# Attention keeps both parts of the split input x in DRAM, and the gated linear attention heads load them

## The chip, the cores and the metric

The kernel runs on one core of a Trainium2 chip. A core has TensorE (PE, the matrix unit), VectorE (DVE), ScalarE (ACT), GpSimd (POOL) and SyncE (SP, which here only issues DMAs); each takes its own instructions in order, and semaphores tie them together. Data lies in on-chip SBUF (128 partitions), matmul results in PSUM, inputs and outputs in DRAM. The metric is device time in microseconds (us); less is better.

## The reference, cut to what matters

One inference layer over 2048 prompt tokens and 64 sample tokens (8 sequences of 8), width 1024, all fp32:

```python
z = jnp.einsum('btd,dn->btn', x, w_in)
q, k, v, g_att, gq, gk, gv, g_gla, g_lr, r_att, r_gla = jnp.split(z, SPLIT_POINTS, axis=-1)
...
    o_att, new_k, new_v = swa_prompt(q, k, v, attn_sink, rel_table)
...
log_a = jax.nn.log_sigmoid((jnp.einsum('btr,rk->btk', g_lr, w_gk_up) + b_gk).astype(jnp.float32)) / GATE_NORMALIZER
o_gla, S = gla(...)
...
h_att = jnp.einsum('bta,ad->btd', o_att * jax.nn.silu(g_att), w_pa)
h_gla = jnp.einsum('btv,vd->btd', o_gla * jax.nn.silu(g_gla), w_pg)
merged = jax.nn.sigmoid(r_att) * h_att + jax.nn.sigmoid(r_gla) * h_gla
y = jnp.einsum('btd,de->bte', merged, w_o)
x = layer_norm(DN_ALPHA * x + y, ln_g, ln_b)
```

`swa_prompt` is attention over a window of 128 with 8 query heads on 2 key heads; `gla` is gated linear attention with 4 heads, keys of 128, values of 256, scanned along the tokens. x is needed for the attention projections, again for those of each GLA head, and again for the merge gates.

## The kernel before

**Numbers.** A product of fp32 accuracy is made of three matmuls in a faster format: an operand is split into a rounded part `hi` and the rest `lo`, and hi·hi, hi·lo and lo·hi are summed in PSUM. `split` (L114 to 116) makes the parts: ACT casts to `hi` (L115), DVE, or POOL where told, subtracts for `lo` (L116). Weights are split too, by `wload` (L125): SP loads a 128x1024 tile into one of two staging buffers (`wst`), ACT makes `wh`, DVE `wl`.

**Stages.** The 2112 tokens are cut into six chunks (`CHUNKS`, L42: four of 384, then 256 and 320, the last with the 64 sample tokens). (1) Attention, L566 to 656: for each chunk the steps k, v, q0 to q3, gl (the low-rank gate), ga0 to ga3 (output gates), each a product (`proj`, L176) of 24 matmuls. After a step, `tick()` runs what a side queue holds for it: the scores, transposes and outputs of the chunk before or of this one. The last chunk's steps also call `wload()`, which brings the GLA weights. (2) GLA, L892 to 972: 4 heads times 6 chunks, each with the gate, values, k, q and two output gates. (3) Merge passes, L1115 to 1242: four passes (`w_pa`, `w_ra`, `w_rg`, `w_pg`) of 7 products of half size with 3 token units each and 4 groups of output rows (p0 to p3). `issue_w` and `issue_x` issue the loads (`ws`, `xc`), `make_w` and `make_x` split them, ahead of the unit that uses them. (4) The output product with layer norm.

**Where x comes from.** x lies transposed in DRAM (`xT`), as eight row tiles of 128. In attention, at ga1, `fetch_x` loads the next chunk's eight tiles, four into `u` units and four into `xst` staging, and at ga2 `part_x` splits them into 16 tiles of tag `x` (of 20); from chunk 1 on, every second subtraction goes to POOL. In GLA the same is done for every head and chunk: `fetch_x` at L939, `part_x` at L963. For the last chunk POOL also copies the sample columns (L158).

**What sets the order.** PE's order is the order of the program (`manual_schedule`, L62); on the other engines the framework's scheduler orders instructions by when they can run. Tile pools decide which SBUF bytes a tile gets, and the first instruction that writes a tile waits for the last users of those bytes. Working tiles come from tags: `u` (29 units of 1.5 KB a partition), `w` (26 of 4 KB), `x`, `xst`, `wst`. The merge stage opens two new pools (L1040): a left one, and a right one that holds `ws`, `xc`, `a12`, `fin`; their tiles lie on what the GLA stage held. PSUM has three `pd` buffers for the projections and five `pa` buffers.

**Names of the prediction.** In the last attention chunk `att_keys` (L334) evicts the k product from its `pd` buffer: ACT makes `kd0` and `kd1` (L340, 341), DVE `kl0` and `kl1` (L343, 344, twice), ACT two more `kd` (L345, 346), and L583 copies `kT`. q1 takes that same buffer. `pT` are transposed probabilities, copied by ACT (L410) and DVE (L408). `gla_store` (L786) writes a head's result `sg` to DRAM, from SP, but for the last chunk of the last head from POOL. The lines around the product and its use of PSUM:

```python
def step(ps_use, w=None):
    if w is not None:
        ps = pd()
        proj(ps[:, :T], w, x, T)
        ps_use(ps[:, :T])
    if last:
        wload()
    tick()
```

Of the kernel before, what the change touches and what calls it, by code (L numbers as in the profile page):

```python
# [12 lines left out]
F32 = mybir.dt.float32  # L13
F32R = mybir.dt.float32r
# [7 lines left out]
P = 128  # L22
D = 1024
# [6 lines left out]
G = 4  # L30
# [13 lines left out]
MT = 352  # L44
MS = NT // (2 * MT)
LB = 384
NU = 29
NX = 20


@with_exitstack
def kernel(ctx, tc, io):
# [17 lines left out]
        return psa.tile([P, 512], F32, tag="pa", name="pa")  # L70

    def wtile(dt=F32, name="w"):
        return sb.tile([P, D], dt, tag="w", name=name, bufs=26)

    def stile(name):
        return sb.tile([P, D], F32, tag="s", name=name, bufs=2)
# [1 line left out]
    def unit(dt=F32, name="u"):  # L78
        return sb.tile([P, TM], dt, tag="u", name=name, bufs=NU)

# [8 lines left out]
    xc_d = dram.tile([4, P, MS, KT // 2, MT], F32, name="xc_d")  # L89
    ac_d = dram.tile([4, P, MS, 2, MT], F32, name="ac_d")  # L90
    uc_d = dram.tile([4, P, MS, KT // 2, MT], F32, name="uc_d")
    gl_d = dram.tile([96, NT], F32, name="gl_d")
    bs_d = dram.tile([NH, P, LB], F32, name="bs_d")

# [19 lines left out]
    def split(dst_h, dst_l, src, eng=nc.vector):  # L114
        pin["a"] = nc.scalar.copy(dst_h, src)  # L115
        i = eng.tensor_tensor(dst_l, src, dst_h.bitcast(F32), ALU.subtract)  # L116
        if eng is nc.vector:
            pin["d"] = i
# [20 lines left out]
            wload()  # L139
        return wready.popleft()  # L140

    def xnew():
        return sb.tile([P, TM], F32R, tag="x", name="x", bufs=NX)

    def xstage():
        return sb.tile([P, TM], F32, tag="xst", name="xst", bufs=4)

    def fetch(src, k, t0, T, stage=xstage):
        st = stage()
        nc.sync.dma_start(st[:, :T], src[:, k, t0:t0 + T])  # L150
        return st, T

    def part(f, new=xnew, eng=nc.vector, samples=False):
        st, T = f
        hi, lo = new(), new()
        split(hi[:, :T], lo[:, :T], st[:, :T], eng)
        if samples:
            nc.gpsimd.tensor_copy(hi[:, T:T + NS], lo[:, T - NS:T])  # L158
        return hi, lo

    def load_split(src, k, t0, T, new):
        return part(fetch(src, k, t0, T), new)

    def fetch_x(src, t0, T):

        return [fetch(src, k, t0, T, unit if k < KT // 2 else xstage) for k in range(KT)]

    def part_x(fs, share=False, samples=False):

        return [part(f, eng=nc.gpsimd if share and k % 2 else nc.vector, samples=samples)  # L170
                for k, f in enumerate(fs)]

    def load_x(src, t0, T, stage=xstage, samples=False):
        return [part(fetch(src, k, t0, T, stage), samples=samples) for k in range(KT)]

    def proj(ps, w, x, T, mid=False):  # L176

# [48 lines left out]
    st, hi, lo = sb.tile([P, D], F32, tag="wst", name="wst", bufs=2), wtile(F32R, "wh"), wtile(F32R, "wl")  # L226
    wseq[0] = 1
    wready.append((hi, lo))
    x = []
    for k in range(KT):  # L230
        if k % 2 == 0:
            cs = slice(k * P, (k + 2) * P)
            nc.sync.dma_start(st[:, cs], io["wt"][0, :, cs])
            split(hi[:, cs], lo[:, cs], st[:, cs])
        x.append(part(fetch(io["xT"], k, *CHUNKS[0], unit)))
    wload(2)


# [314 lines left out]
    for c, (t0, T) in enumerate(CHUNKS):  # L553
        last = c == len(CHUNKS) - 1
        Tp = T - (NS if last else 0)
        nblk = Tp // W
        if last:
            wcap(16)
        A = {"kprev": kprev, "vprev": vprev, "q": [], "sil": []}

        def wt1(key):
            if c == 0:
                W1[key] = wget()
                wload()
            return W1[key]
# [11 lines that stand above are left out]
            gin = gate_in(0, 0)  # L577

        def keys(ps):
            att_keys(A, ps[:, :Tp], Tp)  # L580
            if last:
                A["kT"] = unit(name="kT")
                nc.scalar.copy(A["kT"][:, :T], ps)  # L583

        step(keys, wt1("k"))

        vT = unit(name="vT")
        vt = unit(name="vt").rearrange("p (b c) -> p b c", b=3)
        A["vT"], A["vt"] = vT, vt

        def vtrans(vT=vT, vt=vt, nblk=nblk):
            tp = pa()
            for i in range(nblk):
                nc.tensor.transpose(tp[:, i * P:(i + 1) * P], vT[:, i * P:(i + 1) * P], ident)
            nc.vector.tensor_copy(vt[:, :nblk].rearrange("p b c -> p (b c)"), tp[:, :nblk * P])

        step(lambda ps: nc.scalar.copy(vT[:, :T], ps), wt1("v"))
        at(1, vtrans)
        if c == 0:
            setup0()  # L600
            at(1, setup1)
            at(2, setup2)
            at(4, setup3)

        if last:
            A["qs"] = unit(name="qs")[:, :NB * G * TS].rearrange("p (b g t) -> p b g t", g=G, t=TS)
        for g in range(G):
            def queries(ps, g=g):
                att_queries(A, g, ps[:, :Tp], Tp)
                if last:  # L610
                    nc.scalar.mul(A["qs"][:, :, g, :], ps[:, Tp:].rearrange("p (b t) -> p b t", t=TS), HD ** -0.5)

            step(queries, wt1(("q", g)))

        lag = 2 if c == 0 else 0
        for bi in range(nblk):
            o = lag + 1 + 3 * bi
            at(o, lambda A=A, bi=bi: att_scores(A, bi, 0))
            at(o + 1, lambda A=A, bi=bi: att_scores(A, bi, 1))
            at(o + 3, lambda A=A, bi=bi: att_trans(A, bi, 0))  # L620
            at(o + 4, lambda A=A, bi=bi: att_trans(A, bi, 1))
            at(o + (6 if last and bi else 5), lambda A=A, bi=bi: att_out(A, bi))
        o = lag + 1 + 3 * (nblk - 1) + 5
        if last:
            at(0, lambda A=A, Tp=Tp: samp_rows(A, Tp))
            at(o - 5, lambda A=A, Tp=Tp: samp_prep(A, Tp))
            at(o - 3, lambda A=A: samp_keys(A))
            at(o - 1, lambda A=A, Tp=Tp: samp_scores(A, Tp, 0))
            at(o, lambda A=A, Tp=Tp: samp_scores(A, Tp, 1))
            at(o + 2, lambda A=A, Tp=Tp: (samp_trans(A, 0), samp_trans(A, 1)))  # L630
            at(o + 3, lambda A=A, Tp=Tp: samp_out(A, Tp))
# [12 lines left out]

        for g in range(G):
            sil = unit(name="sil")
            A["sil"].append(sil)
            w = wt1(("ga", g))
            if g == 1:
                with tc.issue_after(pin["w"].ins) if c == 0 else nullcontext():  # L650
                    xf = fetch_x(io["xT"], *CHUNKS[(c + 1) % len(CHUNKS)])
            if g == G - 2:
                xn = part_x(xf, share=(c > 0))
            step(lambda ps: gate(sil, ps, T), w)
        x = xn
        kprev, vprev = (A["k"], T), vt[:, nblk - 1]


# [233 lines left out]
    for h in range(GH):  # L892
        W2 = {}
        wcap(16 + 6 * h)
        for c, (t0, T) in enumerate(CHUNKS):
# [40 lines left out]
                    wload()  # L936
                tick()
            end = last and h == GH - 1
            xf = None if end else fetch_x(io["xT"], *CHUNKS[(c + 1) % len(CHUNKS)])  # L939
            ps = pd()  # L940
            proj(ps[:, :T], wt2("k"), x, T)
            gla_k(B, ps[:, :T])
# [15 lines left out]
            for m in range(2):  # L958
                sg = unit(name="sg")
                B["sg"].append(sg)  # L960
                w = wt2("g", m)
                if m == 0 and not end:
                    xn = part_x(xf, samples=(c + 1 == len(CHUNKS) - 1))  # L963
                ps = pd()
                proj(ps[:, :T], w, x, T, mid=end)
                gate(sg, ps[:, :T], T)
                if len(CHUNKS) - 4 < c < len(CHUNKS) - 1 and m == 1:
                    wload()
                tick()
# [207 lines left out]
    def load_m(t, u, n, last=False, queue=nc.sync):  # L1177
# [7 lines left out]
            out.append((st, n + NS * last))  # L1185
        return out

    def rest_m(t, u, n, last):
        return [part(f, onew, samples=last) for f in load_m(t, u, n, last)]

# [15 lines left out]
    for n, (q, i, s) in enumerate(units):  # L1206
# [16 lines left out]
        for p in range(NP4):  # L1223
# [12 lines left out]
            if n == len(units) - 1:  # L1236
                if p < 3:
                    xr0.append(load_xr(runs(1, p * P, P)))
                x += [part(f, onew) for f in xf[2 * p:2 * p + 2]]
        if n == len(units) - 2:  # L1240

            xf, x, xr0 = load_m(1, 0, TM, queue=nc.scalar), [], []
# [196 lines left out]
```

## Time and profile before

| what | value |
|---|---|
| median of 3 runs (lowest to highest) | 1845.85 us (1841.35 to 1847.47) |
| the profiled execution, its span | 1846.22 us, 1844.4 us |
| mean granted TensorE clock | 0.992 |
| busy: DVE, ACT, POOL | 1280.9 (69%), 849.9 (46%), 422.3 us (23%) |
| DMA | 315.84 MB, mean 171 GB/s |
| the five longest-running groups of matmuls by line: L185, L186, L187, L1233, L1232 | 409.1, 403.5, 403.1, 381.3, 381.4 us |

A row of groups has busy us, mean ns of one, the idle time of the engine just before, and what ended most of it. In a row of waits stand the total, the number of times and the longest. In a timeline row stand start, duration, engine, line, operation, and in brackets the idle time ahead with its releaser. Matmuls are pipelined: where each shows 0.31 us they may start 0.15 us apart, so their pace is read from the starts.

### The profile page before, as it was taken

Reading aid. Unit: us, or ns where it says so; the run is one execution under the profiler, and the core shown is the slowest. Engines: PE = TensorE matmul, PEld = TensorE weight load, DVE = VectorE, ACT = ScalarE, POOL = GpSimd, SP = SyncE. Lnnn points to the kernel's source line nnn. Section 1 sums busy time; section 2 is a strip of 40 time slices with the busy share of each in tenths; the row PEclk is TensorE's granted clock in tenths of the full one; section 3 lists DMA queues with packets and bytes.
Section 4 is the critical chain, followed back from the end, with each engine's and each line's share of the span. In section 5 each row is a group of like instructions: output and inputs, shape, how many; then the busy total and the mean of one; then the engine's idle time right before and its main releaser. Section 6 shows DMA issues by size and latency. Waiting matters only on the chain.

```text
span 1844.4 us, 32399 instructions
## 1 busy us (share of the span) xinstructions
PE 1807.9 (98%) x11683; PEld 1722.2 (93%) x11683; DVE 1280.9 (69%) x2662; ACT 849.9 (46%) x1947; POOL 422.3 (23%) x559
## 2 busy tenths in 40 slices
PE   8999999999999999999999999999999999989997
PEld 7998988899999999999999999999999999988886
DVE  5677778767776776777667669648657566966655
ACT  5444545645665565656546453435443543211110
POOL 3310111300110111011110243430355153631111
PEclk9999999999999999999999999999999999999998
DMA  7211013534345444543543189858887967895531
GB/s 233 63 56 38 12 47 100 165 131 156 120 148 170 143 143 144 186 132 107 181 145 119 58 274 315 283 178 292 276 311 256 310 216 245 287 312 177 166 111 41
DMA packets 199554, 315.84 MB, mean 171 GB/s; under 512 B 21453, under 2 KB 161189, under 8 KB 199376
## 3 DMA queue, kind: packets, MB, share of 16 engines
q1 hardware_dynamic: 192624, 304.61, 50.5%
q0 software_dynamic: 5616, 7.58, 1.5%
q8 instruction: 92, 1.51, 0.3%
q10 hardware_dynamic: 1152, 1.57, 0.3%
q14 instruction: 70, 0.57, 0.1%
HBM read 228.52 MB, written 86.14 MB: 171 GB/s over the span
## 4 chain that ended last, share of the span: by engine, by line
PE 91%; DVE 3%; DMA 3%; issue 1%; POOL 1%; SPq 0%; ACT 0%; DVEq 0%; ACTq 0%; POOLq 0%
PE pd L185 11%; PE pd L187 11%; PE pd L186 11%; PE pa L1234 9%; PE pa L1233 9%; PE pa L1232 9%; PE pd L199 7%; PE pd L198 7%; PE pd L200 7%; PE pa L421 2%; DMA cs<-tt_d 1%; PE pa L406 1%; PE pa L755 1%; PE pa L753 1%; PE pa L754 1%
## 5 line engine op out<-in xcount | busy, mean ns | idle before, releaser
L185 PE MATMUL pd<-x,wh 128*128 128x384 f32 (+2 forms) x1248 | 409.1, 328 | 7.0 <-ACT x L115 6.3
L186 PE MATMUL pd<-x,wh 128*128 128x384 f32 (+2 forms) x1248 | 403.5, 323 | 0.6 <-DVE x L116 0.3
L187 PE MATMUL pd<-x,wl 128*128 128x384 f32 (+2 forms) x1248 | 403.1, 323 | 0.6 <-DVE wl L116 0.6
L1233 PE MATMUL pa<-xl,wh 128*128 128x352 f32 x1176 | 381.3, 324 | 7.9 <-DVE xl L116 7.6
L1232 PE MATMUL pa<-xh,wh 128*128 128x352 f32 x1176 | 381.4, 324 | 2.6 <-ACT xh L115 2.3
L1234 PE MATMUL pa<-xh,wl 128*128 128x352 f32 x1176 | 381.9, 325 | 0.0
L185 PEld LDWEIGHTS pd<-x,wh 128*128 128x128 f32 x1248 | 236.5, 190 | 17.2 <-issue 8.9
L186 PEld LDWEIGHTS pd<-x,wh 128*128 128x128 f32 x1248 | 236.5, 190 | 2.0 <-DVE x L116 1.5
L187 PEld LDWEIGHTS pd<-x,wl 128*128 128x128 f32 x1248 | 236.1, 189 | 1.0 <-DVE wl L116 1.0
L1233 PEld LDWEIGHTS pa<-xl,wh 128*128 128x128 f32 x1176 | 222.7, 189 | 10.4 <-DVE xl L116 10.1
L1232 PEld LDWEIGHTS pa<-xh,wh 128*128 128x128 f32 x1176 | 222.5, 189 | 3.6 <-ACT xh L115 2.6
L1234 PEld LDWEIGHTS pa<-xh,wl 128*128 128x128 f32 x1176 | 224.5, 191 | 0.0
L116 DVE TENSOR_TENSOR xl<-xs,xh 128x1408 fp32r<-128x1408 f32 x63 | 110.5, 1753 | 69.4 <-ACT xh L115 35.7
L198 PE MATMUL pd<-wh,x 128*128 128x256 f32 x512 | 147.9, 289 | 0.0
L199 PE MATMUL pd<-wh,x 128*128 128x256 f32 x512 | 145.6, 284 | 1.2 <-DVE x L116 1.1
L200 PE MATMUL pd<-wl,x 128*128 128x256 f32 x512 | 144.6, 282 | 0.0
L115 ACT CAST x<-xst 128x384 fp32r<-128x384 f32 (+2 forms) x164 | 78.2, 485 | 139.9 <-PE pd L199 117.9
L115 ACT CAST xh<-xs 128x1408 fp32r<-128x1408 f32 x63 | 86.5, 1372 | 103.9 <-PE pa L1234 81.7
L746 POOL TENSOR_SCALAR sq<-sq 128x1 f32<-128x1 f32 (+1 forms) x68 | 21.4, 314 | 467.2 <-ACT ring L745 467.2
L199 PE MATMUL pd<-woh,x 128*128 128x512 f32 x256 | 101.5, 396 | 0.0
L198 PE MATMUL pd<-woh,x 128*128 128x512 f32 x256 | 101.5, 396 | 0.0
L200 PE MATMUL pd<-wol,x 128*128 128x512 f32 x256 | 101.5, 396 | 0.0
(318 smaller groups left out, 3683.6 us busy)
## 6 DMA issues: line engine op xcount, KB each, us to landing
wst<-wt SPq DMA_DIRECT2D x33, 512.0 KB, 3.6
xs<-xc_d SPq DMA_DIRECT2D x24, 704.0 KB, 5.6
cs<-tt_d SPq DMA_DIRECT2D x48, 352.0 KB, 4.7
u<-xT SPq DMA_DIRECT2D x84, 192.0 KB, 4.0
xst<-xT SPq DMA_DIRECT2D x76, 192.0 KB, 2.6
xs<-xT SPq DMA_DIRECT2D x18, 704.0 KB, 5.9
ws<-w_ra SPq DMA_DIRECT2D x36, 256.0 KB, 4.4
ws<-w_rg SPq DMA_DIRECT2D x36, 256.0 KB, 5.6
```

The lines of the kernel that those rows point to most:

```text
L115: pin["a"] = nc.scalar.copy(dst_h, src)
L116: i = eng.tensor_tensor(dst_l, src, dst_h.bitcast(F32), ALU.subtract)
L185: mm(ps, hi[:, s], xh[:, :T], start=(k == 0), stop=False)
L186: mm(ps, hi[:, s], xl[:, :T], start=False, stop=False)
L187: mm(ps, lo[:, s], xh[:, :T], start=False, stop=(k == n - 1))
L198: mm(ps, xh[:, xs], hi, start=(k == 0), stop=False)
L199: mm(ps, xl[:, xs], hi, start=False, stop=False)
L200: mm(ps, xh[:, xs], lo, start=False, stop=(k == KT - 1))
L421: mm(ot[pr, :], vb[:, pr], A["pT", bi, kv][:, hf], start=(hf == h0), stop=(hf == 1))
L1232: mm(ps, wh[:, ks], xh[:, ts], start=(k == 0), stop=False)
L1233: mm(ps, wh[:, ks], xl[:, ts], start=False, stop=False)
L1234: mm(ps, wl[:, ks], xh[:, ts], start=False, stop=(k == q.kh - 1))
```

## The change

x is split once, in attention, and its parts are stored to DRAM (`xs_d`, one tensor a chunk); GLA loads them.

- A slot of tag `x` is now 6 KB a partition and holds the `hi` and `lo` parts of two row tiles; there are 8 slots in place of 20 tiles (`NX`). `fetch_x` brings a chunk's raw x into two such slots (tag `x`, four row tiles each, by four DMAs), and `part_x` splits pair by pair. All subtractions are on DVE. The `xst` staging tag is gone from this stage.
- `keep_x`, called after the k step of each attention chunk, stores the four slots (4 DMAs of 768 KB for a chunk of 384).
- `load_x` takes the place of `fetch_x` and `part_x` in GLA, and of the last attention chunk's fetch: four DMAs of both parts.
- `u` units go from 29 to 24, `w` tiles from 26 to 25.
- `part` moves to the output stage, unchanged.

PE's instructions and their order are the same in both kernels.

```diff
-NU = 29
-NX = 20
+NU = 24
+NX = 8
+def xwide(c):
+    return 2 * CHUNKS[c][1] + (NS if c == len(CHUNKS) - 1 else 0)
...
-        return sb.tile([P, D], dt, tag="w", name=name, bufs=26)
+        return sb.tile([P, D], dt, tag="w", name=name, bufs=25)
...
+    xs_d = [dram.tile([4, P, 2 * xwide(c)], F32, name=f"xs{c}_d") for c in range(len(CHUNKS))]
...
+    def xslot(dt, name):
+        return sb.tile([P, 4 * TM], dt, tag="x", name=name, bufs=NX)
+    def xnew(c):
+        T, n = CHUNKS[c][1], xwide(c)
+        t = xslot(F32R, "x")[:, :2 * n]
+        v = t.rearrange("p (k w) -> p k w", k=2)
+        return t, v[:, :, :n - T], v[:, :, n - T:]
...
+    def fetch_x(c):
+        t0, T = CHUNKS[c]
+        out = []
+        for k in range(0, KT, 4):
+            st = xslot(F32, "xst")[:, :4 * T].rearrange("p (k t) -> p k t", k=4)
+            for j in (0, 2):
+                nc.sync.dma_start(st[:, j:j + 2], io["xT"][:, k + j:k + j + 2, t0:t0 + T])
+                out.append(st[:, j:j + 2])
+        return out
+    def part_x(c, sts):
+        T = CHUNKS[c][1]
+        out = []
+        for st in sts:
+            t, hi, lo = xnew(c)
+            split(hi[:, :, :T], lo, st)
+            if c == len(CHUNKS) - 1:
+                nc.gpsimd.tensor_copy(hi[:, :, T:], lo[:, :, T - NS:])
+            out.append((t, hi, lo))
+        return out
+    def keep_x(c, x):
+        for i, (t, _, _) in enumerate(x):
+            nc.sync.dma_start(xs_d[c][i], t.bitcast(F32))
+    def load_x(c):
+        out = []
+        for i in range(KT // 2):
+            t, hi, lo = xnew(c)
+            nc.sync.dma_start(t.bitcast(F32), xs_d[c][i])
+            out.append((t, hi, lo))
+        return out
...
         step(keys, wt1("k"))
+        keep_x(c, xs)
...
-                    xf = fetch_x(io["xT"], *CHUNKS[(c + 1) % len(CHUNKS)])
-            if g == G - 2:
-                xn = part_x(xf, share=(c > 0))
+                    xn = load_x(0) if last else fetch_x(c + 1)
+            if g == G - 2 and not last:
+                xn = part_x(c + 1, xn)
...
-            xf = None if end else fetch_x(io["xT"], *CHUNKS[(c + 1) % len(CHUNKS)])
+            if not end:
+                xn = tiles(load_x((c + 1) % len(CHUNKS)))
...
-                if m == 0 and not end:
-                    xn = part_x(xf, samples=(c + 1 == len(CHUNKS) - 1))
```

**The order of instructions.** In a row stand the line, the operation, output<-inputs with buffer numbers, and the shape. First ACT in the last attention chunk, before: `pd_3561` is the k product's PSUM buffer, `wh_3689` the next weight cast, `pd_3661` the v product.

```order
L392 ACTIVATE es_3538<-es_3538 128x4
L340 CAST kd0_3586<-pd_3561 64x256
L341 CAST kd1_3587<-pd_3561 64x256
L410 COPY pT_3615<-pa_3616 128x512
L345 CAST kd0_3586<-pd_3561 64x256
L346 CAST kd1_3587<-pd_3561 64x256
L583 COPY kT_3607<-pd_3561 128x320
L115 CAST wh_3689<-wst_3687 128x1024
L390 ACTIVATE s_3628,sm_3642<-s_3628,nm_3641 128x256 x4
L392 ACTIVATE es_3643<-es_3643 128x4
L597 COPY vT_3659<-pd_3661 128x320
```

The same place of the changed kernel (`pd_3429` is the k product, `pd_3533` the v product):

```order
L420 ACTIVATE es_3511<-es_3511 128x4
L122 CAST wh_3561<-wst_3559 128x1024
L122 CAST wh_3609<-wst_3607 128x1024
L438 COPY pT_3613<-pa_3614 128x512
L122 CAST wh_3660<-wst_3658 128x1024
L368 CAST kd0_3454<-pd_3429 64x256
L369 CAST kd1_3455<-pd_3429 64x256
L373 CAST kd0_3454<-pd_3429 64x256
L374 CAST kd1_3455<-pd_3429 64x256
L611 COPY kT_3475<-pd_3429 128x320
L626 COPY vT_3531<-pd_3533 128x320
```

The eviction of the k product (five rows) has moved behind three weight casts and a copy of transposes. On DVE in the changed kernel, the subtractions that belong to it stand so:

```order
L123 TENSOR_TENSOR wl_3610<-wst_3607,wh_3609 128x1024
L436 COPY pT_3613<-pa_3620 128x512
L123 TENSOR_TENSOR wl_3661<-wst_3658,wh_3660 128x1024
L371 TENSOR_TENSOR kl0_3456<-pd_3429,kd0_3454 64x256
L372 TENSOR_TENSOR kl1_3457<-pd_3429,kd1_3455 64x256
L371 TENSOR_TENSOR kl0_3456<-pd_3429,kd0_3454 64x256
L372 TENSOR_TENSOR kl1_3457<-pd_3429,kd1_3455 64x256
```

They too have come behind the subtractions for those weights, and behind the copy of the transposes.

Next, SP at the end of GLA and the start of the merge passes, before; in brackets stand the semaphores that a row waits for (DMAHW: DMAs issued by SP, DMASW: DMAs issued by POOL). The first `ws` is the weight of group p0, the next three those of p1 to p3.

```order
L788 DMA ug3_d_75<-sg_13005 128x256 [waits DMAHW0_49,DVE_49]
L788 DMA ug3_d_75<-sg_13098 128x256 [waits DMAHW1_49,DVE_49]
L1045 DMA xc_13590<-ua_d_71 128x2x352 [waits PE_49,DMAHW2_49,Activation_49,Pool_49]
L1014 DMA ws_13592<-w_pa 128x256 [waits DMAHW3_49]
L1014 DMA ws_13594<-w_pa 128x256 [waits DMAHW4_49]
L1014 DMA ws_13596<-w_pa 128x256 [waits DMAHW5_49]
L1014 DMA ws_13598<-w_pa 128x256 [waits DMAHW6_49]
L1045 DMA xc_13600<-ua_d_71 128x2x352 [waits DMAHW7_49]
L1045 DMA xc_13602<-ua_d_71 128x2x352 [waits DMAHW0_49]
```

The same place of the changed kernel:

```order
L817 DMA ug3_d_75<-sg_11925 128x256 [waits DMAHW4_49,DVE_49]
L817 DMA ug3_d_75<-sg_11978 128x256 [waits DMAHW5_49,DVE_49]
L1073 DMA xc_12470<-ua_d_71 128x2x352 [waits DMAHW5_49,DMASW7_49,DMAHW6_49,PE_49,Activation_49]
L1042 DMA ws_12472<-w_pa 128x256 [waits DMASW6_49,DMAHW7_49,DMASW4_49,Pool_49]
L1042 DMA ws_12474<-w_pa 128x256 [waits DMASW5_49,DMAHW0_49,DMASW0_49,DVE_49]
L1042 DMA ws_12476<-w_pa 128x256 [waits DMAHW1_49,DMASW3_49,DMAHW3_49,Activation_49,Pool_49]
L1042 DMA ws_12478<-w_pa 128x256 [waits DMAHW2_49,PE_49]
L1073 DMA xc_12480<-ua_d_71 128x2x352 [waits Activation_49]
L1073 DMA xc_12482<-ua_d_71 128x2x352 [waits DMAHW4_49,DMASW1_49]
```

The order is the same, but the tiles lie on other tiles' bytes, so the waits differ. That for DMASW5 in the row of `ws_12474` is the landing of a store that POOL issues at the end of GLA, `ug3_d<-sg_12312` (L817), the last head's last chunk.

More of the change, by code (lines that the diff above doesn't have):

```diff
@@ L140, in wget @@
         return wready.popleft()
[L142 to L174, printed above, removed]
+    def xslot(dt, name):
+        return sb.tile([P, 4 * TM], dt, tag="x", name=name, bufs=NX)
@@ new lines, in xnew, with fetch @@
+    def xnew(c):
[3 more added lines that the diff above has]
+        return t, v[:, :, :n - T], v[:, :, n - T:]
+    def fetch(k, T, st):
+        nc.sync.dma_start(st[:, :T], io["xT"][:, k, :T])
+        return st
+    def fetch_x(c):
[7 more added lines that the diff above has]
+        return out
@@ L176, in proj, with tiles @@
+    def tiles(x):
+        return [(hi[:, j], lo[:, j]) for _, hi, lo in x for j in range(2)]
     def proj(ps, w, x, T, mid=False):
@@ L228 @@
     wready.append((hi, lo))
-    x = []
+    xs = []
     for k in range(KT):
@@ L234 @@
             split(hi[:, cs], lo[:, cs], st[:, cs])
-        x.append(part(fetch(io["xT"], k, *CHUNKS[0], unit)))
+            xs.append(xnew(0))
+        st_x = fetch(k, TM, unit())
+        split(xs[-1][1][:, k % 2, :], xs[-1][2][:, k % 2, :], st_x)
+    x = tiles(xs)
     wload(2)
@@ L650 @@
                 with tc.issue_after(pin["w"].ins) if c == 0 else nullcontext():
-                    xf = fetch_x(io["xT"], *CHUNKS[(c + 1) % len(CHUNKS)])
-            if g == G - 2:
-                xn = part_x(xf, share=(c > 0))
+                    xn = load_x(0) if last else fetch_x(c + 1)
+            if g == G - 2 and not last:
+                xn = part_x(c + 1, xn)
             step(lambda ps: gate(sil, ps, T), w)
-        x = xn
+        x, xs = tiles(xn), xn
         kprev, vprev = (A["k"], T), vt[:, nblk - 1]
@@ L1186, in load_m, with part @@
         return out
+    def part(f, samples=False):
+        st, n = f
+        hi, lo = onew(), onew()
+        split(hi[:, :n], lo[:, :n], st[:, :n])
+        if samples:
+            nc.gpsimd.tensor_copy(hi[:, n:n + NS], lo[:, n - NS:n])
+        return hi, lo
     def rest_m(t, u, n, last):
-        return [part(f, onew, samples=last) for f in load_m(t, u, n, last)]
+        return [part(f, last) for f in load_m(t, u, n, last)]
     for tag, n, bufs in (("a12", T, 12), ("fin", T, 6), ("xc", 2 * T, 5), ("ws", KT // 2 * P, 11), ("top", 640, 1),
@@ L1238 @@
                     xr0.append(load_xr(runs(1, p * P, P)))
-                x += [part(f, onew) for f in xf[2 * p:2 * p + 2]]
+                x += [part(f) for f in xf[2 * p:2 * p + 2]]
         if n == len(units) - 2:
```

## Prediction

> **What bounds the kernel now.** I read the page's busy shares and its chain first, then a table of windows, then the list of what PE waits for.
>
> ```profile
> span 1844.4 us, 32399 instructions
> PE 1807.9 (98%) x11683; PEld 1722.2 (93%) x11683; DVE 1280.9 (69%) x2662; ACT 849.9 (46%) x1947; POOL 422.3 (23%) x559
> PE 91%; DVE 3%; DMA 3%; issue 1%; POOL 1%; SPq 0%; ACT 0%; DVEq 0%; ACTq 0%; POOLq 0%
> ```
>
> PE is busy 98% of the span and makes 91% of the chain that ended last. The profiled execution took 1846.22 us, the span of 1844.4 plus 1.8 around it, and stands 0.4 us above the median of 1845.85.
>
> ```profile
> 0.00:50.00 50.00, 41.36 (x195) 36.44 (x196) 29.00 (x46) 25.07 (x42) 18.11 (x44) 0.93 0.73 237
> 300.00:350.00 50.00, 48.45 (x324) 43.15 (x324) 37.96 (x82) 25.40 (x70) 15.61 (x32) 1.00 0.52 156
> 400.00:450.00 50.00, 50.00 (x346) 49.87 (x345) 33.47 (x85) 23.71 (x64) 6.34 (x14) 1.00 0.51 167
> 600.00:650.00 50.00, 50.00 (x354) 49.87 (x353) 36.72 (x90) 28.61 (x72) 5.84 (x12) 1.00 0.46 151
> 1050.00:1100.00 50.00, 46.24 (x279) 43.67 (x279) 29.75 (x64) 23.86 (x59) 17.21 (x23) 0.93 0.79 257
> ```
>
> Columns: the stretch, busy us of PE, its weight loads, DVE, ACT, POOL, then granted clock, DMA share, GB/s. In the GLA heads (windows 400 and 600) PE has no gap at all. Where it has gaps is the start, the last attention chunk (300 to 350) and the step from GLA to the merge passes (1050 to 1100). So work taken off ACT and DVE in GLA buys nothing by itself; the time is decided at those three places.
>
> ```profile
> PE pd L185 <- ACT x L115: 6.3, 3, 4.9
> PE pa L421 <- DVE pT L408: 1.1, 1, 1.1
> PE pd L199 <- DVE x L116: 1.1, 2, 0.7
> PE pd L186 <- POOL x L116: 0.2, 1, 0.2
> ```
>
> Columns: total, times, longest. These are PE's waits on a split of x, and one on a probability tile. The first row lies wholly in the kernel's first loads, which stay.
>
> **The change, part by part.**
>
> *Splits removed in GLA.*
>
> ```profile
> L115 ACT CAST x<-xst 128x384 fp32r<-128x384 f32 (+2 forms) x164 | 78.2, 485 | 139.9 <-PE pd L199 117.9
> ```
>
> Most of these casts, and as many DVE subtractions, go. All of it lay beside a PE that is 50.00 of 50 busy: 0 us. What goes with it are the waits on x inside GLA and the last attention chunk (1.1 + 0.2), and the 1.1 on pT, because the DVE work ahead of that copy moves away (next part). Together **-2.4 us**; bounds 0 to -3, since little more than these rows is there to be had.
>
> *Loads added in GLA.* Each GLA chunk reads 4 tiles of up to 768 KB, where it read 8 of up to 192 KB.
>
> ```profile
> xs<-xc_d SPq DMA_DIRECT2D x24, 704.0 KB, 5.6
> wst<-wt SPq DMA_DIRECT2D x33, 512.0 KB, 3.6
> ```
>
> The nearest load lands in 5.6 us. The slots were freed by the chunk before, and the load is issued one chunk ahead. 24 chunks lie between about 355 and 1055 us, some 29 us each, and DMA is at 0.46 to 0.51 there. Even four loads end to end take 22 us: 0 us; without that cover some 5 us a chunk. DVE's split of one pair now comes after ga3's first matmuls in attention; the nearest shapes are these, twice as wide:
>
> ```profile
> L116 DVE TENSOR_TENSOR xl<-xs,xh 128x1408 fp32r<-128x1408 f32 x63 | 110.5, 1753 | 69.4 <-ACT xh L115 35.7
> L115 ACT CAST xh<-xs 128x1408 fp32r<-128x1408 f32 x63 | 86.5, 1372 | 103.9 <-PE pa L1234 81.7
> ```
>
> Half of 1.37 and 1.75 is 1.6 us, and ga3's rest and the next chunk's first three pairs (over 5 us of PE) lie ahead of its first use: 0 us, bounds 0 to 1 at each of five boundaries.
>
> *Start.* Four stores of 768 KB (the kept parts of chunk 0) go between weight loads on SP. At the 237 GB/s of the first window 3.1 MB are 13 us of DMA time, against 27% of 50 us (13.5) that is idle. I take **+0.5 us**, bounds 0 to 4.
>
> *Last attention chunk: an eviction moved back.* In the changed order ACT evicts k's PSUM tile only after the weight cast `wh_3660`, which stands behind `pT_3613`, the copy of transposes that PE makes after q0; and DVE has the subtraction `wl_3661` ahead of the four `kl`. PE's q1 needs that PSUM buffer, as there are three and k, v, q0 hold them. Before, k was evicted 5 to 9 us ahead of q1. First PE, then ACT, then DVE:
>
> ```profile
> 317.91 1.03 PE L406 MATMUL pa<-ident,s 128*128 128x128 f32 x8
> 318.70 0.39 PE L185 MATMUL pd<-x,wh 128*128 128x320 f32 x1
> ```
>
> ```profile
> 309.17 0.35 ACT L340 CAST kd<-pd 64x256 fp32r<-64x256 f32 x1
> ...
> 312.54 0.36 ACT L345 CAST kd<-pd 64x256 fp32r<-64x256 f32 x1 [2.02 <-DVE kl L344]
> ...
> 313.32 0.42 ACT L583 COPY kT<-pd 128x320 f32<-128x320 f32 x1
> ...
> 320.22 0.59 ACT L410 COPY pT<-pa 128x512 f32<-128x512 f32 x1
> 320.82 1.05 ACT L115 CAST wh<-wst 128x1024 fp32r<-128x1024 f32 x1
> ```
>
> ```profile
> 310.77 0.41 DVE L343 TENSOR_TENSOR kl<-pd,kd 64x256 fp32r<-64x256 f32 x1
> ...
> 312.08 0.43 DVE L344 TENSOR_TENSOR kl<-pd,kd 64x256 fp32r<-64x256 f32 x1
> ...
> 320.56 1.22 DVE L116 TENSOR_TENSOR wl<-wst,wh 128x1024 fp32r<-128x1024 f32 x1
> ```
>
> The transposes end at 317.91 + 1.03 = 318.94, q1 starts 0.24 before that. Now q1 waits for pT 0.59, wh 1.05, wl 1.22, four kl (310.77 to 312.51, 1.74), then kd, kd, kT (312.54 to 313.74, 1.20): 5.8 us, and with the 0.24 about 6.0; some overlap at each hop takes 0.2 off: 5.8. v's and q0's evictions queue behind k's on ACT; q2 and q3 want those a product later, which covers them. The load of `wh_3660`'s staging tile can lengthen it: SP issues it once `wl_3562` has freed the staging buffer, some 5 us before the cast wants it; it lands 3.6 later in the median and has x loads ahead of it. PE restarting after such a stop may run slow at first. In this trace the stretch after the thin work before 1063 does:
>
> ```profile
> 1063.54 0.66 PE L1233 MATMUL pa<-xl,wh 128*128 128x352 f32 x1 [1.43 <-DVE xl L116]
> ...
> 1065.22 0.49 PE L1232 MATMUL pa<-xh,wh 128*128 128x352 f32 x1
> ...
> 1069.03 0.45 PE L1233 MATMUL pa<-xl,wh 128*128 128x352 f32 x1
> ...
> 1069.48 0.32 PE L1232 MATMUL pa<-xh,wh 128*128 128x352 f32 x1
> 1069.64 0.33 PE L1233 MATMUL pa<-xl,wh 128*128 128x352 f32 x1
> ```
>
> 13 matmuls from 1065.22 to 1069.03 are 0.29 each, then 0.16. A slow stretch of 5.8 us loses 2.6. No row shows a warm PE stopped for 6 us, so the bounds are 0 and 2.6, and I take half, 1.3. Sum **+7.1 us**, bounds 4.6 to 9.4. [...]
>
> *Start of the merge passes.* SBUF is laid out anew, and the second group's weight tile (`ws_12474`, for p1) now lies on what held GLA's last `sg`. SP therefore waits for the last GpSimd store to land, with p2's and p3's weights and the x tiles of units 1 and 2 queued behind. Before, SP had issued all four weights early:
>
> ```profile
> 1053.17 1.90 SPq L1014 DMA_DIRECT2D ws<-w_pa  x4
> ...
> 1062.84 1.09 POOL L788 DMA_DIRECT2D ug_d<-sg  x2
> ...
> DMA to landing us min/median/max: 5.0/5.8/6.5
> ...
> ws<-w_pa SPq DMA_DIRECT2D x36, 128.0 KB, 3.8
> xc<-ua_d SPq DMA_DIRECT2D x9, 352.0 KB, 5.3
> ...
> 1061.23 1.32 ACT L115 CAST wh<-ws 128x256 fp32r<-128x256 f32 x4
> ```
>
> The third row is that store's. With SP silent I take its fastest, 5.0: 1067.8. The weight lands 3.0 later (below the 3.8, as DMA is less loaded), its cast takes 0.33: p1 starts at 1071.2 in place of 1065.22, +6.0. The slow stretch starts over, so p0's six matmuls are not warmed on: 6 x 0.13 = 0.8, taken as 0.7. **+6.7 us**. Bounds: a store as quick as the 3.6 of a 512 KB load and half of 3.8 for the weight give +3.4; 6.5 for the later store, and a weight as slow as the 5.3 of an x tile, give +10.8. Unit 1's x is issued at 1069.2, lands at 1074.5, is split by 1076.1; PE reaches it at 1071.2 + 18 x 0.29 = 1076.5: just covered.
>
> **Sum:** -2.4 + 0.5 + 7.1 + 6.7 = +11.9 on 1846.2: 1858.1 profiled, 1857.7 on the median.
>
> **Rivals.**
>
> *One of the two stops doesn't bite, or both are short* (the clock doesn't drop and the store lands at once). Only the attention stop: 1845.85 - 2.4 + 0.5 + 7.1 = 1851.0; only the merge stop: 1850.6; both at their low ends: 1845.85 - 2.4 + 0.5 + 4.6 + 3.4 = 1852.0. Against it: ACT, DVE and SP take their instructions in order, and both waits stand in that order. 0.17.
>
> *Not slower: PE's pace in GLA is held down by the splits' traffic,* and rises without them. Over GLA's 700 us, 1.7% pays the 11.9 back.
>
> ```profile
> 429.20 0.28 PE L200 MATMUL pd<-wl,x 128*128 128x256 f32 x1
> 429.32 0.28 PE L198 MATMUL pd<-wh,x 128*128 128x256 f32 x1
> ```
>
> Here, with DVE busy, a matmul of 256 columns starts every 0.12 us, 0.47 ns a column; at 1069.48, before ACT or DVE have resumed, 352 columns take 0.16, 0.46 ns. Were the 2% between them such a hold and not the rounding, 14 us would go, and the time would be 1843.7. I give it 0.05. [...]
>
> *Loads starve GLA's weights.* SP's queue holds 3 MB of x ahead of weight loads at a head's start; 2 us more at each of three heads give 1863.7, and more is open. DMA at half load speaks against: 0.08.
>
> *The change doesn't do what it says:* attention would still split per GLA head. The instruction rows of ACT and DVE in GLA are gone, so no chance is kept.
>
> **How the numbers follow.** Forecast 0.70, rivals 0.17, 0.05, 0.08. The predicted time is 1857.7. The range is 1848 to 1867: below lies the faster rival and the case of both stops nearly hidden; above lies the merge stop at its upper bound with a late weight load, or the starved heads. 0.3% is 5.5 us, about what a measurement of this kernel can tell from no change. Slower than 1851.4: the forecast, nearly all of it, the starved case and a little of the first rival, 0.76. Within: most of the first rival and the forecast's low end, 0.18. Faster than 1840.3: 0.06, the pace rival and an unseen gain.
>
> **What would show it.** In the changed profile: PE idle of 4.5 to 8 us before the 320-column q1 product near 318 us, put down to ACT `kT`; a first run of matmuls behind it at about twice 0.15 us if the clock drops; PE idle of 3 to 10 us after the first six merge matmuls, put down to `wh`, with SP's `ws` issued only after the POOL store lands; windows 400 to 1000 unchanged at 50.00 with fewer DVE and ACT us; no PE wait on x after 350 us. I am wrong if q1 or p1 start without a gap, or if GLA's windows shift by more than a microsecond or two.

## The result, and the profile after

The changed kernel takes 1860.01 us (median of 4 runs, 1859.41 to 1864.71), beside 1845.48 for the kernel before: a ratio of 1.0083, with an interval of 1.0060 to 1.0106. It is slower by some 15 us. The profiled execution took 1860.13 us, its span is 1858.4.

PE's waits in the changed kernel (total, times, longest), those rows on which the argument rests. In the kernel before, `wh` had 0.3 and `brow` 0.8, and the other three have no row:

```profile
PE pd L210 <- ACT kT L611: 7.9, 1, 7.9
...
PE pa L1268 <- ACT wh L122: 4.4, 2, 4.1
...
PE pa L330 <- DVE rbl L318: 1.3, 1, 1.3
PE pa L329 <- DVE rbh L317: 1.2, 1, 1.2
PE pa L329 <- ACT brow L334: 1.2, 1, 1.2
```

The waits on x in the last attention chunk and at GLA's start are gone; three new places wait. By windows (busy us of PE, its loads, DVE, ACT, POOL, granted clock, DMA share, GB/s):

```profile
0.00:50.00 50.00, 39.85 (x166) 34.77 (x167) 25.84 (x42) 22.60 (x38) 14.37 (x37) 0.90 0.79 271
...
300.00:350.00 50.00, 42.11 (x287) 37.88 (x286) 30.86 (x75) 23.29 (x62) 6.26 (x17) 0.93 0.51 178
350.00:400.00 50.00, 49.64 (x387) 45.11 (x387) 32.82 (x91) 23.32 (x70) 7.59 (x16) 1.00 0.37 116
400.00:450.00 50.00, 50.00 (x407) 49.56 (x406) 27.45 (x73) 23.71 (x58) 4.18 (x9) 1.00 0.70 252
600.00:650.00 50.00, 50.00 (x356) 49.84 (x355) 29.65 (x74) 24.16 (x57) 4.82 (x11) 1.00 0.56 199
...
1050.00:1100.00 50.00, 42.10 (x263) 38.94 (x262) 28.73 (x72) 20.35 (x54) 12.76 (x21) 0.90 0.55 179
```

In GLA, DVE has 6 to 7 us less in 50 than before and PE is at 50.00, as it was in these two windows. The loss lies in the windows at 0, 300 and 1050.

Since PE runs the same matmuls in the same order, the same matmul can be looked up in both traces, and the difference of its start times tells how far the changed kernel is behind there:

| matmul | before, us | after, us | behind by |
|---|---|---|---|
| the 137th, in the first chunk | 39.80 | 44.87 | 5.1 |
| transposes ahead of q1, last attention chunk | 317.91 | 319.92 | 2.0 |
| q1's first | 318.70 | 328.84 | 10.1 |
| q1's tenth | 320.11 | 331.40 | 11.3 |
| the last of merge group p0 | 1064.92 | 1074.30 | 9.4 |
| the first of p1 | 1065.22 | 1078.93 | 13.7 |
| one 235 matmuls further | 1104.92 | 1119.48 | 14.6 |
| end of span | 1844.4 | 1858.4 | 14.0 |

So 5.1 us come in at the start, 3.1 are won back up to q1, 9.3 are lost at q1 (a stop, then slow matmuls), 1.9 are won from there to the end of GLA and 5.2 are lost at the start of the merge passes. Behind that the difference still wanders (11.4 at 1485 us of the kernel before, 13.7 at 1700), so the last row is good to a few us only.

**The stop at q1.** PE, then ACT, then DVE of the changed kernel (start, duration, and in brackets the idle time with its releaser):

```profile
319.92 1.04 PE L434 MATMUL pa<-ident,s 128*128 128x128 f32 x8
328.84 0.64 PE L210 MATMUL pd<-x,wh 128*128 128x320 f32 x1 [7.89 <-ACT kT L611]
...
331.40 0.46 PE L210 MATMUL pd<-x,wh 128*128 128x320 f32 x1
...
331.85 0.31 PE L212 MATMUL pd<-x,wl 128*128 128x320 f32 x1
```

```profile
320.80 0.58 ACT L438 COPY pT<-pa 128x512 f32<-128x512 f32 x1
323.58 1.05 ACT L122 CAST wh<-wst 128x1024 fp32r<-128x1024 f32 x1 [2.21 <-DMA wst<-wt]
324.54 0.36 ACT L368 CAST kd<-pd 64x256 fp32r<-64x256 f32 x1
...
327.58 0.36 ACT L373 CAST kd<-pd 64x256 fp32r<-64x256 f32 x1 [2.30 <-DVE kl L372]
...
328.36 0.42 ACT L611 COPY kT<-pd 128x320 f32<-128x320 f32 x1
```

```profile
324.66 1.23 DVE L123 TENSOR_TENSOR wl<-wst,wh 128x1024 fp32r<-128x1024 f32 x1 [1.91 <-ACT wh L122]
325.81 0.41 DVE L371 TENSOR_TENSOR kl<-pd,kd 64x256 fp32r<-64x256 f32 x1
```

This is the chain of the prediction, step by step: pT, the weight cast, DVE's subtraction for that weight, four `kl`, two `kd`, kT. It has one more link, the 2.21 us in which ACT waits for the weight's load to land. SP issued that load as soon as DVE had freed the staging buffer (318.03 + 1.22 = 319.25), 2.1 us before ACT was ready to cast (320.80 + 0.58 = 321.38):

```profile
319.28 6.96 SPq L138 DMA_DIRECT2D wst<-wt  x3
```

Behind the stop nine matmuls take (331.40 - 328.84) / 9 = 0.28 us each, where 0.15 is the pace a moment later: 1.2 us more.

**The start of the merge passes.** PE, POOL with the landing of its stores, SP, ACT:

```profile
1074.30 0.49 PE L1270 MATMUL pa<-xh,wl 128*128 128x352 f32 x1
1078.93 0.66 PE L1268 MATMUL pa<-xh,wh 128*128 128x352 f32 x1 [4.13 <-ACT wh L122]
...
1082.32 0.48 PE L1270 MATMUL pa<-xh,wl 128*128 128x352 f32 x1
...
1082.81 0.32 PE L1269 MATMUL pa<-xl,wh 128*128 128x352 f32 x1
```

```profile
1072.22 1.10 POOL L817 DMA_DIRECT2D ug_d<-sg  x2
```

```profile
DMA to landing us min/median/max: 3.0/3.1/3.2
```

```profile
1064.03 13.56 SPq L1042 DMA_DIRECT2D ws<-w_pa  x4
```

```profile
1078.48 0.75 ACT L122 CAST wh<-ws 128x256 fp32r<-128x256 f32 x2 [7.46 <-DMA ws<-w_pa]
```

SP's four weight loads, 1.90 us of queue time before, now stretch over 13.56, because the second waits for the POOL store. That is issued by 1072.8 and lands 3.1 later, at 1075.9; the weight is cast at 1078.48.

**The start.** The four stores of chunk 0's parts stand between the weight loads on SP, and ACT waits for weights:

```profile
12.50 0.91 SPq L188 DMA_DIRECT2D xs_d<-x  x2
...
16.41 1.64 SPq L188 DMA_DIRECT2D xs_d<-x  x2
```

```profile
27.73 1.05 ACT L122 CAST wh<-wst 128x1024 fp32r<-128x1024 f32 x1 [3.91 <-DMA wst<-wt]
```

In the kernel before, the cast of the same weight starts 5.3 us earlier:

```profile
22.42 1.05 ACT L115 CAST wh<-wst 128x1024 fp32r<-128x1024 f32 x1
```

DMA is full while the stores move. From 15 to 25 us, the changed kernel first, then the kernel before (the last two columns are DMA share and GB/s):

```profile
15.00:20.00 5.00, 4.36 (x24) 4.04 (x24) 4.25 (x8) 1.98 (x3) 0.00 (x0) 1.00 1.03 399
20.00:25.00 5.00, 4.68 (x27) 4.36 (x26) 1.72 (x3) 2.48 (x4) 0.00 (x0) 1.00 0.99 409
```

```profile
15.00:20.00 5.00, 4.36 (x24) 4.04 (x25) 4.65 (x8) 2.29 (x5) 0.00 (x0) 1.00 0.44 125
20.00:25.00 5.00, 5.00 (x31) 5.00 (x30) 3.02 (x5) 4.22 (x8) 0.00 (x0) 1.00 0.59 190
```

DVE's `rbh` and `rbl` are ordered behind that weight's split, and PE waits for them and for `brow`: 3.7 us by the first list, where the kernel before had 0.8 (`brow`).

### The profile page after: what moved, and what is told of

It is laid out like the page before. It is cut to its first block, busy times and chain, and to the rows that moved or that the text cites. A ratio compares the mean times of both kernels' runs of the same rounds, so it can differ in the third digit from the quotient of the medians.

```text
span 1858.4 us, 31579 instructions
## 1 busy us (share of the span) xinstructions
PE 1809.5 (97%) x11683; PEld 1721.9 (93%) x11683; DVE 1196.7 (64%) x2470; ACT 770.0 (41%) x1735; POOL 391.2 (21%) x511
## 4 chain that ended last, share of the span: by engine, by line
PE 86%; DMA 6%; DVE 4%; issue 1%; ACT 1%; POOL 1%; SPq 0%; DVEq 0%; POOLq 0%; ACTq 0%
PE pd L210 11%; PE pd L211 10%; PE pd L212 10%; PE pa L1269 8%; PE pa L1268 8%; PE pa L1270 8%; PE pd L225 6%; PE pd L223 6%; PE pd L224 6%; DMA wst<-wt 2%; DMA cs<-tt_d 2%; PE pa L449 1%; PE pa L434 1%; PE pa L783 1%; PE pa L784 1%
## 5 line engine op out<-in xcount | busy, mean ns | idle before, releaser
L1269 PEld LDWEIGHTS pa<-xl,wh 128*128 128x128 f32 x1176 | 222.9, 190 | 12.0 <-DVE xl L123 11.9
L123 DVE TENSOR_TENSOR wl<-ws,wh 128x512 fp32r<-128x512 f32 (+1 forms) x112 | 86.9, 787 | 23.2 <-ACT wh L122 22.6
```

The lines of the kernel that those rows point to most:

```text
L1269: mm(ps, wh[:, ks], xl[:, ts], start=False, stop=False)
```

## The experiments

**1. The eviction's place (evict).** In the instruction order of the changed kernel the eviction stands directly behind the load of `gin`, a tile that `gate_in` takes from the same pool of units just ahead of `kd0`. On the chip that load was issued at 307 and landed 10.0 us later, 7.5 us before `kd0` ran (324.54), so it isn't what held `kd0` there; the order was. The edit moves two lines of the program:

```diff
-        if last:
-            gin = gate_in(0, 0)
         def keys(ps):
...
         step(keys, wt1("k"))
+        if last:
+            gin = gate_in(0, 0)
```

> The changed kernel, with gate_in(0, 0) called behind the k step of the last attention chunk in place of ahead of it; k's eviction then stands on ACT right behind one weight cast, 9 us earlier. Theory (the eviction's place in ACT's order makes the stop at q1): the wait of 7.9 us on kT falls below 1, with it the slow matmuls behind it (1.2 us), so about 9 us less: 1851. Rival (late weight loads, which queue behind the x loads, are what ACT really waits for): PE stops at q1 or q2 all the same, and at most 3 us go: 1857 or more.

Measured: 1852.15 us, ratio to before 1.0049 (1.0035 to 1.0063), where the changed kernel has 1.0083. In the trace q1's tenth matmul comes 10.1 us earlier than in the changed kernel, and no wait on kT is left. The theory holds. A smaller wait is new, at which PE loses 1.7 us:

```profile
PE pa L622 <- ACT vT L625: 1.5, 1, 1.5
```

**2. The layout (layout).** The order in which the right pool's tags are first made sets where they lie:

```diff
-    for tag, n, bufs in (("a12", T, 12), ("fin", T, 6), ("xc", 2 * T, 5), ("ws", KT // 2 * P, 11), ("top", 640, 1),
+    for tag, n, bufs in (("xc", 2 * T, 5), ("fin", T, 6), ("ws", KT // 2 * P, 11), ("a12", T, 12), ("top", 640, 1),
```

> The changed kernel, with the tags of the right merge pool laid out in the order xc, fin, ws, a12, top, so that the first x and weight tiles lie on bytes that GLA freed long before, and only a12 on the last sg. Theory (SP waits for GpSimd's last store before p1's weight): the wait of 4.1 us on wh falls to 0.3, p1 starts 4 to 5 us earlier: 1855. Rival (those loads, or the clock, would have held p1 anyway): under 1.5 us less: 1858.5 or more.

Measured: 1854.84 us, ratio 1.0062 (1.0048 to 1.0076). From p0's last matmul to p1's first no time is lost:

```profile
1072.60 0.49 PE L1270 MATMUL pa<-xh,wl 128*128 128x352 f32 x1
1072.90 0.49 PE L1268 MATMUL pa<-xh,wh 128*128 128x352 f32 x1
```

Against the changed kernel the lead grows by 4.3 us from p0's last matmul to p1's first (from 1.7, the spread of two executions up to there, to 6.0). The theory holds.

**3. The stores of chunk 0 (keep).**

```diff
-        keep_x(c, xs)
+        if c:
+            keep_x(c, xs)
...
+            if c == 0 and g == 1:
+                with tc.issue_after(pin["w"].ins):
+                    keep_x(c, xs)
             step(lambda ps: gate(sil, ps, T), w)
```

> The changed kernel, with the four stores of chunk 0's parts issued at ga1 of chunk 0, behind the last weight load, in place of behind the k step. Theory (the stores share DMA time and SP's queue with the weight loads of the start): rbh, rbl and brow are no longer late, PE is 4.5 us ahead by 40 us, and keeps it: 1855.5. Rival 1 (one weight tile less, 25 for 26, delays the weights): no difference, 1860. Rival 2 (the stores then hold x slots that chunk 1 needs): 2 us or more come back as waits on x near 75 us: 1857.5 or more.

Measured: 1855.66 us, ratio 1.0066 (1.0052 to 1.0079). The 136th matmul starts 4.6 us earlier than in the changed kernel (44.55 to 39.91), and 4.7 us of lead are there at q1's first (328.84 to 324.10): no wait comes back in chunk 1. The weight cast that had waited 3.91 us now runs at

```profile
22.68 1.05 ACT L122 CAST wh<-wst 128x1024 fp32r<-128x1024 f32 x1 [0.24 <-DMA wst<-wt]
```

with 25 weight tiles as in the changed kernel, so rival 1 falls.

**4. Queue or DMA engines (keepq).** The same stores at their old point, from another queue:

```diff
-            nc.sync.dma_start(xs_d[c][i], t.bitcast(F32))
+            (nc.scalar if c == 0 else nc.sync).dma_start(xs_d[c][i], t.bitcast(F32))
```

> The changed kernel, with chunk 0's four stores issued at the same point but from ACT's DMA queue in place of SP's. Theory A (the weight loads stand behind the stores in one queue): the loads pass, PE is 3 us or more ahead of the changed kernel at 40 us. Theory B (the 16 DMA engines are full, whatever the queue): the loads are as late, PE gains under 1.5 us there.

Measured, in a single execution: 1855.18 us; the 131st matmul, at 42.95 in the changed kernel, starts 2.9 us earlier, the 137th 3.7. The same weight cast:

```profile
24.68 1.05 ACT L122 CAST wh<-wst 128x1024 fp32r<-128x1024 f32 x1 [2.05 <-DMA wst<-wt]
```

It is 3.0 us earlier than in the changed kernel and 2.0 later than without the stores there. So the larger part of the 5 us goes with the order in one queue (theory A); that the rest is the load on the DMA engines is likely, and not shown. How large each part is stays rough. In evict and layout, whose start is that of the changed kernel, the 137th matmul starts at 44.14 and 43.76 in place of 44.87, and against these keepq gains 3.0 and 2.6. The edit also moves the stores in time: ACT issues them between its casts, at 9.33, 14.05, 17.17 and 21.68, where SP issued them from 12.50 to 18.05.

**5. All three edits (all3).**

> The three edits together: gate_in behind the k step, right merge pool in the order xc, fin, ws, a12, top, chunk 0's stores at ga1. Theory (three separate delays, which add up): 9 + 4.5 + 4.5 = 18 us less than the changed kernel, 1842, which is 3.5 below the kernel before, the size of its waits on x and pT in the last attention chunk (2.4) and a little of its start. Rival (the delays overlap, or a next wait stands behind each): 1846 to 1850, not below the kernel before.

Measured: 1842.83 us, where the kernel before has 1842.89 in the same runs: ratio 0.9993 (0.9982 to 1.0005). The three delays add up, as the theory had it: 0.0090 of the ratio is 16.6 us against the 18 expected, good to some 5 us by the two intervals. By their own ratios the three edits give 6.3, 3.9 and 3.1 us; their intervals all reach into that of the changed kernel, so the proof of each edit is in its trace. But the result lies on the kernel before, not 3.5 below it. PE's wait in the last chunk:

```profile
PE pa L623 <- ACT vT L626: 1.5, 1, 1.5
```

**6. Where gate_in stands (all3q, all3g).** The wait on vT sits behind `gate_in` too: vT's eviction is the next one in the program that takes a unit. In all3q, `gate_in` stands behind the four q steps (out of the loop); in all3g behind q1:

```diff
             step(queries, wt1(("q", g)))
+            if last and g == 1:
+                gin = gate_in(0, 0)
```

> The three edits, with gate_in behind the four q steps in place of behind the k step, so that v's eviction (vT) stands on ACT ahead of two weight casts. Theory: the wait of 1.5 us on vT, which the earlier place brought in, goes, and nothing else is late: 1.5 us less than the three edits, about 1841, 1.5 to 2.5 below the kernel before. Rival (another wait takes its place, or the gate's load is late at GLA's start): equal to the three edits, and equal to the kernel before.

Measured: 1848.09 us beside 1845.05, ratio 1.0017 (1.0003 to 1.0032), above the 0.9993 of all3, with intervals that just touch. The expectation failed, in a telling way: the wait on vT is gone, and a stop as long as that on kT stands a few steps further on:

```profile
PE pd L210 <- DVE gl L123: 8.2, 1, 8.2
```

`gl` is the next tile of units behind `gate_in`; its split is again late, and PE's ga2 wants its PSUM buffer (gl, ga0 and ga1 hold the three).

> The three edits, with gate_in behind the q1 step of the last attention chunk, where by the instruction orders no eviction that PE waits for stands behind it. Theory (the stop goes wherever gate_in stands ahead of an eviction that PE needs: kT in the changed kernel, vT with it behind k, gl with it behind q3): no wait of PE over 0.6 us between 300 and 400 us, and 8 us less than all3q in the profile there; 1.5 to 4 us below the kernel before. Rival (the pairs and their eight slots bring a stop of their own into the last chunk): a wait of 1.5 us or more stays there, and the time is not below the kernel before.

Measured: 1842.51 us beside 1843.44, ratio 0.9993 (0.9978 to 1.0007). The windows show that no stop is left in the last attention chunk and at GLA's start, where the kernel before had 48.45 and 48.93:

```profile
300.00:350.00 50.00, 50.00 (x351) 46.00 (x350) 36.42 (x85) 26.16 (x74) 11.58 (x25) 1.00 0.54 187
350.00:400.00 50.00, 50.00 (x450) 46.01 (x449) 29.09 (x87) 25.84 (x69) 1.52 (x3) 1.00 0.59 200
```

So the first theory holds: the stop follows `gate_in`. The gain that it was to bring isn't clear of zero. In the trace all3g is 8.9 us ahead of the kernel before at 1028 us, 5.5 at 1113, 2.3 at 1485, and 2.3 behind at 1700; but this was the slowest of its 12 executions (1848.71), and where a typical one loses its lead isn't settled.

**7. The round trip by itself (resplit, resplitg, nosplit).** resplit and resplitg are all3q and all3g without `keep_x` and `load_x`; GLA fetches and splits x per head:

```diff
-                    xn = load_x(0) if last else fetch_x(c + 1)
-            if g == G - 2 and not last:
-                xn = part_x(c + 1, xn)
+                    xn = fetch_x((c + 1) % len(CHUNKS))
+            if g == G - 2:
+                xn = part_x((c + 1) % len(CHUNKS), xn)
...
-                xn = tiles(load_x((c + 1) % len(CHUNKS)))
+                xn = fetch_x((c + 1) % len(CHUNKS))
...
                 w = wt2("g", m)
+                if m == 0 and not end:
+                    xn = tiles(part_x((c + 1) % len(CHUNKS), xn))
```

> The kernel of all3q (pairs of row tiles in 8 slots, the same places of the edits), but without the stores of the parts and their loads: each GLA head loads x and splits it, as the kernel before did. What is left of the difference is the round trip through DRAM alone. Theory (PE has no gap in GLA that the splits make): within 2 us of all3q; PE windows 400 to 1000 at 50.00. Rival (the splits do hold GLA back where 8 slots leave pairs waiting): 4 us or more slower than all3q.

Measured: 1850.31 us, ratio 1.0030 (1.0018 to 1.0042), beside 1.0017 (1.0003 to 1.0032) for all3q: 2.2 us between the medians, with intervals that overlap, and the 8.2 us stop on `gl` in both. This pair doesn't decide.

> The kernel of all3g without the round trip: no stores of the parts, and each GLA head loads x and splits it, as the kernel before did. Theory (the splits lay beside a busy PE): within 2.5 us of all3g, either side, with PE at 49.9 or more of 50 in the windows from 400 to 1000 us in both. Rival (the round trip itself is worth something once its side effects are gone): 4 us or more slower than all3g.

Measured: 1842.94 us, ratio 0.9998 (0.9985 to 1.0010), beside 1842.51 and 0.9993 for all3g. 0.4 us apart: with the side effects gone, the kernel with the round trip and the one without it take the same time, as far as intervals of some 2.5 us to either side can tell. The windows of GLA, resplitg first, then all3g:

```profile
400.00:450.00 50.00, 50.00 (x338) 49.81 (x337) 33.85 (x78) 22.57 (x54) 5.14 (x13) 1.00 0.49 157
```

```profile
400.00:450.00 50.00, 50.00 (x339) 49.81 (x338) 29.72 (x73) 19.22 (x49) 5.33 (x12) 1.00 0.58 197
```

4 us of DVE and 3 of ACT less in 50, 40 GB/s more, PE the same.

nosplit is the kernel before with neither loads nor splits of x in GLA:

> The kernel before, with no loads of x and no splits of x in GLA: all heads and chunks work on the parts of chunk 0 that the last attention chunk made, so the values are those of other tokens. It is the upper bound of what taking the splits out of GLA can give. Theory: only the two waits on x at GLA's start could go, which stem from attention's split and stay: 0, within 1.5 us of the kernel before. Rival (ACT's, DVE's and DMA's work slows PE): 5 us or more below it.

Measured: 1843.25 us beside 1845.05, ratio 0.9986 (0.9972 to 1.0000). That is a little over the 1.5 of the theory, and the interval, from nothing to 5 us, excludes neither. The trace says more: against the kernel before, nosplit's matmuls go from 0.8 us ahead at 350 us to 3.4 ahead at 1028, so some 2.6 us are what GLA gave. Of these 1.9 come in small steps at seven places from 510 us on, and between them the pace is the same. At six of the seven the kernel before shows PE's weight load waiting for a split of x, for 0.16 to 0.25 us, too short for the list of waits:

```profile
510.24 0.19 PEld L199 LDWEIGHTS pd<-wh,x 128*128 128x128 f32 x1 [0.24 <-DVE x L116]
```

The changed kernel wins the same 1.9 us at the same seven places, and so do resplit and resplitg, which still split x in GLA (resplitg loses 0.8 elsewhere). So splitting by pairs in the new slots gives this gain as well, without the round trip; the 3.1 us won up to q1 are there in resplitg too (1.8 ahead at the 137th matmul, 4.9 at q1).

## Why the prediction was right, step by step

The forecast was slower, +11.9 us on the profiled execution; it came +13.9 (1846.22 to 1860.13), inside the range and with the two stops that it named. Term by term, up to 1105 us, the forecast missed by -2.6 (waits), +4.6 (start), +2.2 (q1) and -1.5 us (merge). These partly cancel, so that the total came this near is in part luck.

- *Splits removed in GLA, 0 us.* Right to within what was measured: taking the splits out gives 1.8 us in nosplit (1845.05 to 1843.25, from nothing to 5 by its interval) and 0.4 between resplitg and all3g. But "no gap at all" was read from two windows at 50.00, and the seven short waits above, 1.9 us in sum, don't show there.
- *Waits removed, -2.4.* Measured -3.1 up to q1 (5.1 behind to 2.0), of which 2.2 at the copy of pT, and about -1.9 more by the end of GLA, so the bound of -3 was passed. For pT the list had 1.1, its idle time alone; by the starts, the eight products there run 2.2 us closer together.
- *Start, +0.5.* This term was mis-sized: +5.1 in this profile (4.3 and 4.0 in those of evict and layout, which start alike), at or above its bound of 4. I weighed the stores as 13 us of DMA time against the 13.5 that lie idle in 50 us; but they are issued from 12.50 to 18.05 us, and from 15 to 25 us DMA then is full (share 1.03 and 0.99). keep showed that the cost goes when the stores stand behind the weights, and keepq that the larger part of it is their place in SP's queue, ahead of the weights that the first chunk waits for.
- *Stop at q1, +7.1 (bounds 4.6 to 9.4).* Right in mechanism, +9.3 measured. The chain was sized at 5.8 and PE waited 7.9; the 2.21 of ACT's wait for the weight's load is the difference, which the prediction had named and left at nothing: it had that load issued 5 us before the cast, and SP issued it 2.1 before. The bounds of 4.6 and 9.4 stand there without a sum. The slow matmuls behind the stop cost 1.2 against 1.3 taken.
- *Start of the merge passes, +6.7 (bounds 3.4 to 10.8).* Right in mechanism, +5.2 measured, of which 4.1 is the stop. The store landed in 3.1 us, where I took the 5.0 of the trace before, whose DMA share is 0.79 from 1050 to 1100 us against 0.55 here.
- *Loads in GLA, 0 us.* Right: PE at 50.00 in every window from 400 to 1000 us, with DMA at 0.52 to 0.70.

The slow matmuls come after stops of 7.9, 8.2 and 4.1 us and last 2.8, 3.4 and 3.7 us (to 331.67, from 349.77 to 353.14 in all3q, to 1082.62); no such stretch lasted the 5.8 us from which the prediction took half. The granted clock was 0.50 from 328.84 to 331.67 and from 1078.93 to 1082.62, and 0.99 in the 2 and 3 us behind each. What sets how long such a stretch lasts is not shown. That the prediction's 1.3 us came out near the 1.2 measured at q1 is luck, since it is half of a stretch that did not occur.

Of the rivals, none came about. The pace of PE's matmuls in GLA did not rise without the splits (but for the seven waits they start at the same distances in nosplit as before), and GLA's weights weren't starved.

## What to carry to other kernels

Here, work taken off engines that run beside a busy PE was worth no more than the short waits that it ended (1.9 us); what the change cost was decided by what it moved: the order that a scheduler writes down for the other engines (9.3 us at q1), the bytes that the next stage's first tiles lie on (5.2), and bulk stores that are put into the queue of loads someone waits for (5.1). Two of the three were read from the instruction orders and their waits before a run, and the third stood in SP's order too: look for each PSUM buffer's eviction and each stage's first loads, and for what now stands ahead of them. A cheap edit at each place (a line moved, tags in another order, a store issued later) took the whole loss back.

## What the runs showed that I had not expected

The order of evictions hung on the place of a prefetch. Moving `gate_in`, whose load of `gin` POOL issues and whose tiles nothing reads before GLA starts, moved an 8 us stop from kT to gl, shortened it to 1.5 us at vT, or removed it. evict differs from the changed kernel, and all3, all3q and all3g from each other, by that place alone. Why the order is written so stays open. `gate_in` and the evictions take units from one pool, but it also loads and splits `wgk` with SP, ACT and DVE. And the kernel before calls it at the same point as the changed one, without a stop on kT; that its 29 units against 24 make the difference is likely, and no run tried it.

The pace of a long run of equal matmuls differs in steps between profiled executions. The same 1901 merge matmuls, with no waits, took 304.2 us in the profile of before (1181.28 to 1485.44) and 302.0 in that of after (1194.77 to 1496.81). Over all twelve profiles only three values occur: 302.0 (after, evict, keep, keepq, all3, nosplit), 304.2 (before, resplit) and 306.3 (layout, all3q, all3g, resplitg), 1.4% from lowest to highest. With one profile of each kernel, it is open whether the kernel or the execution sets the step. It is as much as the gains looked for in all3 and all3g, and no kernel here that does the whole computation beat the kernel before by more than its interval.
